# A gated DeltaNet scan with its chunk transitions formed ahead, on quarters of the array

## The chip, the cores and the metric

The kernel runs on one core of a Trainium2 chip. A core has a matrix engine (TensorE, PE in the profile), three engines for elementwise work (VectorE or DVE, ScalarE or ACT, GpSimd or POOL) and queues of DMA transfers. PE writes into PSUM, from which VectorE and ScalarE read; in this kernel POOL works on SBUF alone. The metric is the device time of one execution in microseconds: the median of several runs.

## The reference

Two layers of a transformer block over 256 context and 512 latent tokens of width 1024. Each layer modulates its input, projects it, sends parts of the projection through three mixers (a gated MLP over chunks, attention, a bidirectional gated DeltaNet), projects back, normalizes, and runs an MLP. The change is in the DeltaNet: 6 heads of 64 channels, run over the tokens in chunks of 64, once forward and once backward. For a head and a direction:

```python
sol = lax.linalg.triangular_solve(eye + lower, rhs, ...)     # rhs = [v * beta, k * beta * exp(gc)]
u, w = jnp.split(sol, 2, -1)
def step(s, inp):
    qd, kd, u_i, w_i, a_i, gl = inp
    v_new = u_i - w_i @ s
    o = qd @ s + a_i @ v_new
    s = s * jnp.exp(gl)[..., None, None] + kd.T @ v_new
    return s, o
s_final, o = lax.scan(step, state, xs)
```

`s` is the 64x64 state of the head, `gc` the running sum of the log decay in the chunk, `gl` its last value, `a_i` the masked and decayed product of queries and keys of the chunk. All is float32. The second layer needs no outputs for the context tokens.

## The kernel before

**Stages.** A layer runs an input projection with the gated MLP, then the projections of DeltaNet and attention (304 us ends that stage in layer 0, about 1458 us in layer 1), then a stage in which attention and the DeltaNet scans run side by side (304 to 576 us and 1458 to 1672 us, the scan stages below), and then the output projection and the MLP, which fill most of the rest.

**Order.** The kernel is written as streams: Python generators that yield after each step. `Flow.run` puts them into one order at build time: the stream whose last step ends first, by the rough prices of `Flow.cost`, goes on next. Each engine then runs its instructions in that order. A stream asks for PSUM with `self.psum(n)`: up to 512 columns come from four tiles called `mm`, more from two called `ax`. Attention, the modulation and the DeltaNet share them. In the scan stage the streams are `makes(p)` and `scans(p)` for the three head pairs p, the attention, `prep(2)`, and in layer 0 `mods` (products `modw,cz`).

**DeltaNet.** Heads go in pairs p = 0, 1, 2. Token tiles have 128 tokens, two chunks each. `dn_prep` (p) makes, for all six tiles, the decayed products of queries and keys (`A`) and the transposed inverses of the unit-triangular systems (`TT`). The inverse rests on a long serial chain of small VectorE operations on `Xx` and `tm`. `prep(0)` and `prep(1)` run beside the projections, `prep(2)` in the scan stage.

The scan of a pair of heads goes in six step pairs v. A step pair takes forward the two chunks of tile v, and backward the two of tile `_tb(v)`. So there are 18 step pairs in a layer, 36 in all. 30 of them also give outputs (need: all of layer 0, and v over 1 in layer 1). `dn_make` gets the operands of a step pair ready, and `dn_scan` runs its two steps.

**dn_make** scales keys and queries by token (`gs`, VectorE), transposes them on PE against `c_ident`, and copies the pieces (ScalarE) into 128x128 blocks `rW` and `rQ`; the keys of the update go into `rK` and half of the increments into `rU` (VectorE), the inverses into `rT` (four DMAs from `TT`), the query products into `rA` (ScalarE). In each block the two directions stand on the diagonal and the rest is zero. `ring` makes the blocks in four copies and clears the zero parts with 160 POOL memsets of 64x128 in all, 80 at the start of each scan stage.

**dn_scan** runs a step as a chain over three engines: PE `S,rW`; VectorE `rr = rU - ...`; PE `rr,rT`; ScalarE copy `vn`; PE `vn,rK`; two VectorE operations that give the next `S`. With need, PE then does `S,rQ` and `vn,rA`, and ScalarE (first direction at a tile) or VectorE (second) puts the result into `o`. Each product is 128x128x128, both heads' columns past each head's weights:

```python
            # both heads move past the weights of each: it keeps the array's clock up, and only a head's own product is used
            for h in range(2):
                mm(px[:, 64 * h : 64 * h + P], c2(r["W"], h), S0, start=True, stop=True)
```

In the trace such a product is two records of the same shape (`S,rW` has 144 products and 288 records); a transpose is one. All operations are issued through a helper, so nearly every record has line L206, and one tells them apart by tile names. `S,rW` is a product of the tiles S and rW; `c_ident,ape` and `ava,apT` are attention's transposes and products with values, `akh,qs` and `akl,qs` its scores, `ax<-kq` products of `dn_prep` on 64x64 quarters of the array.

Of the kernel before, what the change touches and what calls it, by code (L numbers as in the profile page):

```python
# [8 lines left out]
F32 = mybir.dt.float32  # L9
# [7 lines left out]
P = 128  # L17
# [7 lines left out]
NH = 6  # L25
# [14 lines left out]
class Flow:  # L40
    """Interleaves streams of work (generators that yield after each step) as they are traced. The engines run what is
    traced in order, so the stream whose last step ends first, by a rough cost of each instruction, goes on next. A stream
    yields a generator to start it, a key to wait until that key is in `done`, a tuple of classes of PSUM tiles to get,
    or the time to go on."""

    # wait for a result of the same engine, of another one
# [68 lines left out]
    def when(self, s):  # L115
        """the time a stream can go on, None while what it waits for is not there"""
# [11 lines left out]
    def run(self, *gens, side=(), drain=False):  # L128
        """until the streams gens end; those of side go on in the next run if they have not ended, or else with drain"""
# [37 lines left out]
    def step(self, gen, val, ahead):  # L167
        """one step of a stream, its instructions as if they were traced that much earlier"""
# [42 lines left out]
class _Core:  # L211
    """the engines, with a note of all that is issued to them"""
# [6 lines left out]
def _tb(v):  # L219
    """token tile whose chunks the backward direction takes at step pair v (the forward one takes tile v)"""  # L220
# [63 lines left out]
class K:  # L284
# [22 lines left out]
    def setup(self):  # L307
# [21 lines left out]
        nc.vector.memset(self.mhalf, -0.5)  # L329
        self.cz = cp.tile([P, KD, 32], F32, name="cz")  # L330
# [6 lines left out]
        # scratch in DRAM  # L337
# [7 lines left out]
    def store(self, out, in_):  # L345
        """a store, traced when the data is about to be there: loads keep a queue to themselves"""
# [6 lines left out]
    def psum(self, *ns):  # L353
        """PSUM tiles of n columns, to be dropped after their last use"""
# [12 lines left out]
    def feed(self, name, side, srcs, raw, parts, scale=None, hold=""):  # L367
        """a pool for weight units with the stream that loads and splits them"""
# [12 lines left out]
    def rsqrt(self, out, in_, n, scale=1.0, eps=EPS):  # L381
        """out = (in_ * scale + eps) ** -0.5 on [P, n]"""
# [68 lines left out]
    def mod_in(self, wt, bt, bufs):  # L451
        """shift and scale of the first layer's input, one half of the channels after the other"""
# [122 lines left out]
    def norm_act(self, out, x, n):  # L575
        """(x - mean) * rstd on the scalar engine"""
# [41 lines left out]
    def chan(self, unit, xh, xl, rng):  # L618
        """channel-major block: psum [P, tokens] for the token columns of rng"""
# [14 lines left out]
    def tokm(self, units, rows, w, c0, c1, t, xh, xl):  # L634
        """token-major block: psum [P, c1-c0] for token tile t; units[i] holds the k-rows rows[i], each w wide"""
# [31 lines left out]
# channel blocks of each half that the vector engine takes in the first modulation  # L667
# [3 lines left out]
class Kernel(K):  # L671
# [23 lines left out]
    def mix(self, l, xp, xh, xl, rest):  # L695
        """rest: pools of the layer before that its last streams use"""
# [5 lines left out]
        # gMLP: u channel-major, v token-major with the gates of the DeltaNet  # L702
# [75 lines left out]
        # the weights of the next phase come in meanwhile  # L778
# [6 lines left out]
        # DeltaNet: convolutions of all heads, preparation of the first pairs; attention: q, k, v; gate of the DeltaNet  # L785
# [61 lines left out]
        # attention proper beside the scans  # L847
# [14 lines left out]
        def makes(p):  # L862
            yield f"prep{l}{p}"
            yield f"conv{l}{3 * p + 2}"
            for v in range(6):
# [5 lines left out]
        def scans(p):  # L871
# [7 lines left out]
            for v in range(6):  # L879
                yield f"made{l}{p}{v}"  # L880
                yield from self.dn_scan(l, p, v, G, R[p % 2][v % 2], S, o)
# [60 lines left out]
    def att_tab(self, l, at):  # L942
        """rotary tables times the norm gains: [q|k, cos|sin, tile, channel]"""
# [14 lines left out]
    def qk_norm(self, l, t, h0, ps, at):  # L958
        """rms-norm and rotary of the q|k heads h0.. of token tile t, then channel-major"""
# [57 lines left out]
    def z_gate(self, l, t, ps):  # L1017
        """silu(z) times the gain of the DeltaNet's output norm"""
        nc, ap_ = self.nc, self.atmp
        pz, ps = ps, ps[:, 128:512]  # L1020
        if t == self.tiles[0]:
# [15 lines left out]
    def attention(self, l, at):  # L1037
        """scores of a head run ahead of the products of the head before"""
# [97 lines left out]
    def dn_conv(self, l, u, c0, r, qkv):  # L1136
        """q, k or v of a head pair from its projection r: convolution, silu, norms; token-major"""
# [11 lines left out]
        # outputs run over cb columns a..b  # L1149
# [15 lines left out]
        # acc is twice the silu; to token-major  # L1165
# [11 lines left out]
        else:  # L1177
            # sums of squares over the channels of each head
# [7 lines left out]
            # l2 norm of x = acc / 2 with its guard; q also carries 1/8  # L1186
# [15 lines left out]
    def dn_gates(self, l, gt, gp, dp, G):  # L1202
        """decay sums and rates of all heads, [P, direction, tile, head]"""
# [18 lines left out]
        # softplus(x) = max(x, 0) + log(1 + e^-|x|), the log as 2 atanh(e / (2 + e))  # L1222
# [714 lines left out]
```

## Time and profile before

| | |
|---|---|
| median of 3 runs (lowest to highest) | 2101.53 us (2100.57 to 2102.2) |
| span of the profiled execution | 2099.3 us |
| PE busy | 1944.5 us, 93% |
| VectorE busy | 1358.6 us, 65% |
| ScalarE busy | 921.4 us, 44% |
| POOL busy | 195.3 us, 9% |

The span lies 2.2 us under the median. Busy shares are means over stages with different limits, and the busy time of PE counts modelled ends: a group of four records of `vn,rA` has 0.61 us of busy time, while the next group starts 0.44 us after it. So a stretch in which PE shows as nearly full can still hold waits. The profile's windows give busy times and the granted TensorE clock by stretch; 1.00 is 2.4 GHz, 0.50 is 1.2 GHz.

### The profile page before, as it was taken

What the parts mean: (1) busy time and instruction counts of PE and PEld (TensorE: products, weight loads), DVE (VectorE), ACT (ScalarE), POOL (GpSimd) and SP (SyncE); (2) the same over time, 40 slices, a digit from 0 to 9 for tenths busy, and PEclk for the clock granted to TensorE, in tenths of its full rate; (3) what the DMA queues carried; (4) which work ended last, traced back from release to release, by engine and by line L of the source; (5) the groups of instructions that cost most, each with busy time, mean ns of one, the idle gap of its engine ahead of it and who ended that gap; (6) DMA issues with size and microseconds to landing.
All of it is one profiled execution on the core that took longest, in us unless ns stands there. A gap on an engine that the chain in (4) does not pass through costs nothing. (4 is left out here: it accounts for less than half of the span.)

```text
span 2099.3 us, 31005 instructions
## 1 busy us (share of the span) xinstructions
PE 1944.5 (93%) x11870; PEld 1601.5 (76%) x11870; DVE 1358.6 (65%) x2659; ACT 921.4 (44%) x1881; POOL 195.3 (9%) x375
## 2 busy tenths in 40 slices
PE   6999779989898999999999989997988889999998
PEld 2887655678777888888888778875877768788886
DVE  5578887865577436362457777889896485544555
ACT  4444346566645322322232265443866445422341
POOL 1111221010012000000000111122100010000001
PEclk8999989989999999999999979977999999999999
DMA  7311024312335424241445243110101434322231
GB/s 280 103 46 51 16 75 149 117 40 64 112 110 181 132 72 159 81 140 43 139 161 173 98 142 95 53 36 26 34 23 30 166 129 164 107 90 81 96 107 59
DMA packets 98240, 208.91 MB, mean 100 GB/s; under 512 B 30850, under 2 KB 45058, under 8 KB 98092
## 3 DMA queue, kind: packets, MB, share of 16 engines
q1 hardware_dynamic: 86956, 189.24, 27.9%
q10 hardware_dynamic: 11136, 17.70, 2.2%
q8 instruction: 93, 1.52, 0.3%
q14 instruction: 55, 0.45, 0.1%
HBM read 184.38 MB, written 17.79 MB: 96 GB/s over the span
## 5 line engine op out<-in xcount | busy, mean ns | idle before, releaser
L206 ACT ACTIVATE whi<-wraw 128x1024 fp32r<-128x1024 f32 (+2 forms) x188 | 194.9, 1050 | 440.6 <-PE ax L206 287.8
L206 DVE TENSOR_TENSOR wlo<-wraw,whi 128x1024 fp32r<-128x1024 f32 (+2 forms) x188 | 226.4, 1211 | 224.6 <-ACT whi L206 224.1
L206 PE MATMUL mm<-x2xh,whi 128*128 128x256 f32 (+1 forms) x832 | 288.4, 347 | 10.5 <-ACT whi L206 9.0
L206 PE MATMUL mm<-x2xh,wlo 128*128 128x256 f32 (+1 forms) x832 | 287.3, 346 | 1.6 <-DVE wlo L206 1.6
L206 PE MATMUL mm<-x2xl,whi 128*128 128x256 f32 (+1 forms) x832 | 287.7, 346 | 0.0
L206 PE MATMUL ax<-whi,hh 128*128 128x512 f32 x640 | 251.2, 392 | 0.0
L206 PE MATMUL ax<-whi,hl 128*128 128x512 f32 x640 | 250.0, 391 | 0.0
L206 PE MATMUL ax<-wlo,hh 128*128 128x512 f32 x640 | 249.9, 390 | 0.0
L206 PEld LDWEIGHTS mm<-x2xh,whi 128*128 128x128 f32 x832 | 158.9, 191 | 34.1 <-ACT whi L206 9.4
L206 DVE TENSOR_TENSOR acc<-acc,ax 128x1024 f32<-128x1024 f32 x68 | 82.9, 1219 | 148.3 <-PE ax L206 148.1
L206 PEld LDWEIGHTS mm<-x2xh,wlo 128*128 128x128 f32 x832 | 158.6, 191 | 22.6 <-DVE wlo L206 2.4
L206 PEld LDWEIGHTS mm<-x2xl,whi 128*128 128x128 f32 x832 | 158.8, 191 | 19.9
L206 PEld LDWEIGHTS ax<-whi,hh 128*128 128x128 f32 x640 | 120.2, 188 | 29.7 <-ACT hh L206 5.2
L206 PEld LDWEIGHTS ax<-whi,hl 128*128 128x128 f32 x640 | 120.1, 188 | 27.5 <-DVE hl L206 2.9
L206 PEld LDWEIGHTS ax<-wlo,hh 128*128 128x128 f32 x640 | 120.2, 188 | 27.0 <-issue 2.6
L206 ACT ACTIVATE rl<-mm 128x256 f32<-128x256 f32 (+1 forms) x104 | 50.7, 490 | 129.1 <-PE mm L206 123.7
L206 DVE SCALAR_TENSOR_TENSOR acc<-modw,cz,acc 128x1024 f32<-128x1024 f32 x80 | 101.2, 1280 | 8.4 <-DMA acc<-in_mod_b 5.4
L206 POOL TENSOR_SCALAR rs<-mv 128x1 f32<-128x1 f32 x52 | 33.1, 637 | 699.1 <-DVE mv L206 696.8
L206 PE MATMUL mm<-ava,apT 128*128 128x128 f32 x624 | 88.4, 285 | 2.7 <-ACT apT L206 1.2
L206 PEld LDWEIGHTS mm<-ava,apT 128*128 128x128 f32 x624 | 78.8, 197 | 7.2 <-ACT apT L206 3.2
L206 DVE TENSOR_TENSOR hl<-rl,hh 128x768 fp32r<-128x768 f32 (+2 forms) x76 | 54.4, 716 | 29.4 <-ACT hh L206 29.4
L206 DVE SCALAR_TENSOR_TENSOR cacc<-cb,cw,cacc 128x772 f32<-128x772 f32 (+1 forms) x72 | 69.7, 972 | 0.7 <-ACT cacc L206 0.2
(255 smaller groups left out, 4178.5 us busy)
## 6 DMA issues: line engine op xcount, KB each, us to landing
wraw<-in_w_up SPq DMA_DIRECT2D x64, 512.0 KB
wraw<-in_w_down SPq DMA_DIRECT2D x64, 512.0 KB
modw<-in_mod_w SPq DMA_DIRECT2D x56, 512.0 KB
modw<-in_mod_w SPq DMA_DIRECT2D x80, 256.0 KB
wraw<-in_w_ch SPq DMA_DIRECT2D x22, 512.0 KB
wraw<-in_w_out SPq DMA_DIRECT2D x16, 512.0 KB
x_d<-xt ACTq DMA_DIRECT2D x16, 512.0 KB
xt<-x_d SPq DMA_DIRECT2D x14, 512.0 KB
```

The source lines that it names most:

```text
L206: return f(*args, **kw)
```

## The change

The step is rewritten as one product and one addition: s' = P s + C, with the transition P = exp(gl) I - kd' w and the increment C = kd' u, and o = Q s + a u with the reading matrix Q = qd - a w. None of P, C, Q and a u depends on the state.

- `dn_make` scales keys and values on VectorE (`kv`, three operations) and ScalarE (one), and `kd`, `qd` and `ei` (the identity times the decay) on POOL (two operations each, 128x128). PE then does products of 64x64 weights on quarters of the array: `kv,TT` (8 per step pair, 128 columns) gives w and u in one; ScalarE copies them to `rwu`; then `kd,rwu` (8) and `rwu,kd` (8) give P and C, and `id,qd` (8) with `A,rwu` (8, accumulated) give Q, 64 columns each. VectorE adds `ei` (128x256), ScalarE copies C and Q.
- `dn_scan` does `rwu,A` (8) once per step pair, and per step four `S,rP` and, with need, four `S,rQ`, then one 128x128 VectorE addition for `S`. Both steps keep two `mm` tiles. At the end of the step pair ScalarE copies (128x256), VectorE adds (128x256) and POOL puts the two results into `o`.
- The padded blocks, their memsets and the DMAs of `rT` go. `A` becomes one tile, and `dn_prep` writes it with two 128x256 products per group of two token tiles where it had two of 64x256 and four of 64x128.
- `Flow.cost` prices products of 64x64 weights at 0.9 ns a column; the decays `E` come from one product instead of 24 small ones per layer; `makes(2)` waits for the last operands of p = 0; one VectorE operation more in the gates.

```diff
+            if m == 64 and ins[0].shape[0] == 64:
+                return 0.9 * n
...
     def dn_make(self, l, p, v, qkv, G, A, TT, r):
...
-            ps = yield from self.psum(256)
-            for h in range(2):
-                self.tr(ps[:, 128 * h : 128 * h + P], g_[:, h].rearrange("p d e -> p (d e)"))
...
-            nc.sync.dma_start(out=r["T"][f, :, 3 * hf, :], in_=T4[f, 0, v])
...
+        for d, t in enumerate(td):
+            mul(nc.vector, kv[:, d, :, 0, :], k[:, t], ks[:, d, t, hs])
+        nc.scalar.copy(kv[:, 0, :, 1, :], vv[:, v])
+        mul(nc.vector, kv[:, 1, :, 1, :], vv[:, td[1]], be[:, 1, td[1], hs])
+        for d, t in enumerate(td):
+            mul(nc.gpsimd, kd[:, d], k[:, t], kds[:, d, t, hs])
...
+        ps = yield from self.psum(512)
+        for d, h in blk:
+            for f in halves:
+                o = P * (2 * d + h)
+                mm(ps[f, o : o + P], T4[f, d, h, td[d]], kv[f, d, h].rearrange("p a b -> p (a b)"), start=True, stop=True)
...
+        nc.scalar.copy(wu.rearrange("p d h c -> p (d h c)"), ps)
...
+        ps, pc = yield from self.psum(512, 256)
+        for d, h in blk:
+            for i, f in enumerate(halves):
+                mm(ps[f, 256 * d + 64 * h : 256 * d + 64 * h + HD], wu[f, d, h, 0:HD], kd[f, d, h], start=True, stop=True)
+                e = i if d == 0 else 1 - i
+                o = P * e + 64 * h
+                mm(pc[halves[1 - i], o : o + HD], kd[f, d, h], wu[f, d, h, HD:P], start=True, stop=True)
...
+        nc.vector.tensor_tensor(out=r["P"], in0=pv[:, :, 0, :], in1=ei.rearrange("p d h c -> p d (h c)"), op=ALU.add)
+        nc.scalar.copy(r["C"].rearrange("p e c -> p (e c)"), pc)
...
+    def dn_scan(self, l, p, v, A, r, S, o):
...
+            for h, i, f, d in w:
+                c = P * e + 64 * h
+                mm(px[halves[1 - i], c : c + HD], r["P"][f, d, 64 * h : 64 * h + HD], S0[f, h, :], start=True, stop=True)
+            for h, i, f, d in w if need else ():
+                c = 256 + P * d + 64 * h
+                mm(po[f, c : c + HD], r["Q"][f, d, 64 * h : 64 * h + HD], S0[f, h, :], start=True, stop=True)
...
+            nc.vector.tensor_tensor(
+                out=S2.rearrange("p h c -> p (h c)"), in0=px[:, P * e : P * e + P], in1=r["C"][:, e, :], op=ALU.add
+            )
...
+        nc.scalar.copy(yo, y[:, 0])
+        nc.vector.tensor_tensor(out=yo, in0=yo, in1=y[:, 1], op=ALU.add)
...
+                nc.gpsimd.tensor_tensor(out=of[:, t], in0=of[:, t], in1=yo[:, d], op=ALU.add)
```

**PE, late in the scan stage of layer 1.** Before, one step with need stands so, among the scores and transposes of attention:

```order
L206 MATMUL mm_66<-S,rW_12546 128x128 x2
L206 MATMUL mm_68<-c_ident,gs 128x128 x2
L206 MATMUL mm_69<-c_ident,ape 128x128 x2
L206 MATMUL mm_66<-rr,rT_12551 128x128 x2
L206 MATMUL ax_70<-akh,qs 128x512
L206 MATMUL ax_70<-akl,qs 128x512
L206 MATMUL ax_70<-akh,qs 128x256
L206 MATMUL mm_66<-vn,rK_12556 128x128 x2
L206 MATMUL ax_70<-akl,qs 128x256
L206 MATMUL mm_67<-S,rQ_12561 128x128 x2
L206 MATMUL mm_67<-vn,rA_12566 128x128 x2
```

Now both steps of a step pair stand in a few rows, with the products `kv,TT` of a later step pair between them:

```order
L209 MATMUL mm_69<-ava,apT 128x128 x6
L209 MATMUL mm_67<-rwu_12781,A_12797 64x64 x8
L209 MATMUL mm_66<-S,rP_12782 64x64 x4
L209 MATMUL mm_67<-S,rQ_12783 64x64 x4
L209 MATMUL mm_68<-kv,TT_12798 64x128 x8
L209 MATMUL mm_66<-S,rP_12782 64x64 x4
L209 MATMUL mm_67<-S,rQ_12783 64x64 x4
L209 MATMUL mm_69<-c_ident,ape 128x128 x4
```

What moved: the three products that each waited for another engine became one round of quarter products per step, and PE changes between whole-array and quarter products there (110 stretches of 64x64 products in the program, 27 before).

**VectorE, in the projections of layer 1.** Before, a group of two token tiles of `dn_prep` writes `A` in six operations:

```order
L206 TENSOR_TENSOR A_11026<-ax_71,M 64x2x2x64 x2
L206 TENSOR_TENSOR A_11027<-ax_71,DB 64x2x64 x4
L206 TENSOR_TENSOR M<-ax_71,M 128x2x128 x2
L206 SCALAR_TENSOR_TENSOR cacc<-cb_11048,cw,cacc 128x772 x2
L206 TENSOR_TENSOR A_11027<-ax_71,M 64x2x2x64 x2
```

Now in two:

```order
L209 TENSOR_TENSOR A_11269<-ax_70,M 128x2x128
L209 TENSOR_TENSOR A_11269<-ax_70,DB 128x2x128
L209 TENSOR_TENSOR M<-ax_70,M 128x2x128 x2
L209 SCALAR_TENSOR_TENSOR cacc<-cb_11290,cacc 128x512
L209 SCALAR_TENSOR_TENSOR cacc<-cb_11289,cw,cacc 128x772
```

Only the operations on `A` are fewer; the convolution (`cacc`) and `M` stand beside them as before.

**POOL, at the start of the scan stage of layer 1.** Before, the stretch begins with the memsets of the states and of the padded blocks (20 rows of `x4`, of which the first stand here):

```order
L206 MEMSET S_12542 128x128
L206 MEMSET S_12543 128x128
L206 MEMSET rW_12546 64x2x64 x4
L206 MEMSET rT_12551 64x2x64 x4
L206 MEMSET rK_12556 64x2x64 x4
```

Now the operands of the step pairs follow the states:

```order
L209 MEMSET S_12777 128x128
L209 MEMSET S_12778 128x128
L209 MEMSET TT_12798 128x1536
L209 TENSOR_TENSOR kd<-qkv_11263,kds 128x128 x2
L209 TENSOR_TENSOR ei<-id_84,E 128x128 x2
L209 TENSOR_TENSOR qd<-qkv_11263,egc 128x128 x2
L209 TENSOR_TENSOR kd<-qkv_11264,kds 128x128 x2
```

The memsets of the ring are gone, and POOL's products stand where `dn_make` needs them, through the whole stage.

## Rows read from the trace of the kernel before

**Rows 1.** The page of the profile: its first line.

```profile
span 2099.3 us, 31005 instructions
```

**Rows 2.** Windows: stretch, length, PE, PEld, DVE, ACT, POOL busy (records), clock, DMA share, GB/s.

```profile
180.00:304.00 124.00, 105.19 (x711) 83.18 (x709) 108.83 (x240) 45.08 (x78) 18.19 (x19) 0.94 0.11 37
304.00:432.00 128.00, 118.09 (x911) 74.89 (x913) 98.23 (x343) 79.65 (x244) 17.97 (x89) 0.96 0.40 124
432.00:475.00 43.00, 38.66 (x387) 34.34 (x382) 26.04 (x91) 29.50 (x106) 5.09 (x4) 0.80 0.19 52
475.00:576.00 101.00, 92.31 (x717) 84.43 (x715) 56.89 (x169) 65.59 (x180) 2.47 (x2) 1.00 0.28 90
1370.00:1458.00 88.00, 77.63 (x548) 63.68 (x546) 75.10 (x181) 30.50 (x57) 16.81 (x21) 0.82 0.06 23
1458.00:1550.00 92.00, 78.64 (x792) 70.50 (x793) 84.38 (x278) 73.08 (x213) 16.08 (x82) 0.93 0.14 34
1550.00:1672.00 122.00, 99.88 (x895) 88.00 (x895) 74.61 (x242) 71.87 (x209) 5.51 (x6) 0.97 0.22 70
```

**Rows 3.** Records by tile, whole span: count, then duration ns min/median/max.

```profile
L206 PE MATMUL mm<-S,rW x288: 272/275/582, 315.5 to 1642.4; 128*128 128x128 f32 x144
L206 PE MATMUL mm<-S,rQ x240: 272/275/422, 324.7 to 1643.9; 128*128 128x128 f32 x120
L206 PE MATMUL mm<-c_ident,gs x132: 271/273/477, 310.9 to 1634.1; 128*128 128x128 f32 x132
```

**Rows 4.** Timeline of PE, full clock: start us, busy us, group of records.

```profile
377.81 0.61 PE L206 MATMUL mm<-vn,rA 128*128 128x128 f32 x4
378.35 0.66 PE L206 MATMUL ax<-kq 64*64 64x128 f32 x10
378.94 0.71 PE L206 MATMUL mm<-S,rQ 128*128 128x128 f32 x4
379.49 0.61 PE L206 MATMUL mm<-vn,rA 128*128 128x128 f32 x4
...
414.89 0.61 PE L206 MATMUL mm<-S,rW 128*128 128x128 f32 x4
415.33 0.61 PE L206 MATMUL mm<-ava,apT 128*128 128x128 f32 x4
```

**Rows 5.** Groups of instructions, 1458 to 1550 us: count, busy us, mean ns, idle before.

```profile
L206 DVE TENSOR_TENSOR rK<-qkv,kds 64x128 f32<-64x128 f32 x42 | 11.4, 282 | 0.4
L206 DVE SCALAR_TENSOR_TENSOR S<-S,E,mm 128x64 f32<-128x64 f32 x38 | 9.4, 275 | 3.5 <-PE mm L206 2.1 <-ACT o L206 0.6 <-ACT rU L206 0.5
```

**Rows 6.** Timeline of VectorE, one group of `dn_prep` in layer 1's projections.

```profile
1419.60 0.76 DVE L206 TENSOR_TENSOR M<-ax,M 128x256 f32<-128x256 f32 x2
1420.49 0.86 DVE L206 TENSOR_TENSOR A<-ax,M 64x256 f32<-64x256 f32 x2
1421.38 1.20 DVE L206 TENSOR_TENSOR A<-ax,DB 64x128 f32<-64x128 f32 x4
```

**Rows 7.** Waits, 1458 to 1672 us: engine, awaited, us in total, times, longest.

```profile
PE mm L206 <- DVE gs L206: 7.8, 2, 7.6
PE mm L206 <- ACT vn L206: 3.8, 9, 0.9
PE mm L206 <- DVE rr L206: 3.6, 5, 2.1
```

**Rows 8.** Records by tile, POOL, whole span.

```profile
L206 POOL MEMSET rK<- x32: 197/198/201, 306.8 to 1470.9; 64x128 f32 x32
L206 POOL TENSOR_SCALAR rs<-mv x52: 190/430/2252, 22.9 to 2092.4; 128x1 f32<-128x1 f32 x52
```

**Rows 9.** Windows before a fall of the clock and after it, columns as in Rows 2.

```profile
429.00:432.70 3.70, 1.94 (x61) 1.70 (x60) 3.65 (x8) 2.67 (x6) 0.00 (x0) 1.00 0.00 0
433.00:443.00 10.00, 10.00 (x102) 8.64 (x102) 4.92 (x21) 6.86 (x26) 0.00 (x0) 0.50 0.01 3
```

**Rows 10.** Timeline of PE in the second of these windows.

```profile
437.39 1.06 PE L206 MATMUL mm<-S,rW 128*128 128x128 f32 x4
```

More of the change, by code (lines that the diff above doesn't have):

```diff
@@ L329, in setup @@
         nc.vector.memset(self.mhalf, -0.5)
+        self.id2 = cp.tile([P, HD], F32, name="id2")
+        for f in range(2):
+            nc.vector.tensor_copy(self.id2[_half(f)], self.ident[_half(f), 64 * f : 64 * f + HD])
         self.cz = cp.tile([P, KD, 32], F32, name="cz")
@@ L864, in makes @@
             yield f"conv{l}{3 * p + 2}"
+            if p == 2:
+                yield f"made{l}05"
             for v in range(6):
@@ L1020, in z_gate @@
         pz, ps = ps, ps[:, 128:512]
+        yield f"z{l}{t - 1}" if t > self.tiles[0] else f"qk{l}{LT[-1]}"
         if t == self.tiles[0]:
@@ L1249, in dn_gates @@
         gc, egc, kds = (gp.tile(sh, F32, name=n) for n in ("gc", "egc", "kds"))
-        gks = gp.tile([P, 6, NH], F32, name="gks")
+        ks = gp.tile(sh, F32, name="ks")
         ps, pr = yield from self.psum(144, 768)
@@ L1364, in dn_prep @@
         for g in range(3):
-            need = A[g] is not None
+            a0 = 0 if l == 0 else 2
+            need = 2 * g >= a0
             nq = 2 if need else 1
@@ L1513, in dn_make @@
-        if A is not None:
-            yield from rows("Q", q, egc[:, 1])
-            for hf, f in halves:
-                nc.scalar.copy(r["A"][f, :, hf:4:2, :], A[f, v % 2])
-            yield
-    def dn_scan(self, l, p, v, G, r, S, o):
+        mul = lambda eng, o, a, s: eng.tensor_tensor(out=o, in0=a, in1=_col(s, HD), op=ALU.mult)
+        halves = [_half(f) for f in range(2)]
+        blk = [(d, h) for d in range(2) for h in range(2)]
+        mm = nc.tensor.matmul
+        T4 = TT.rearrange("p (d h t) c -> p d h t c", d=2, h=2)
@@ new lines, in dn_make @@
+        if need:
+            qd = new("qd", 2, 2, HD)
+            for d, t in enumerate(td):
+                mul(nc.gpsimd, qd[:, d], q[:, t], egc[:, d, t, hs])
+            yield
+        ei = new("ei", 2, 2, HD)
+        for d, t in enumerate(td):
+            nc.gpsimd.tensor_tensor(
+                out=ei[:, d], in0=self.id2.unsqueeze(1).broadcast_to([P, 2, HD]), in1=_col(E[:, d, t, hs], HD), op=ALU.mult
+            )
+        yield
+        ps = yield from self.psum(512)
[3 more added lines that the diff above has]
+                mm(ps[f, o : o + P], T4[f, d, h, td[d]], kv[f, d, h].rearrange("p a b -> p (a b)"), start=True, stop=True)
@@ new lines, in dn_make @@
+        for d, h in blk if need else ():
+            o = 256 * d + P + 64 * h
+            for f in halves:
+                mm(ps[f, o : o + HD], qd[f, d, h], self.id2[f], start=True, stop=False)
+            for f in halves:
+                mm(ps[f, o : o + HD], wu[f, d, h, 0:HD], A[f, d, h, td[d] - a0], start=False, stop=True)
+        yield
+        pv = ps.rearrange("p (d w c) -> p d w c", d=2, w=2)
+        nc.vector.tensor_tensor(out=r["P"], in0=pv[:, :, 0, :], in1=ei.rearrange("p d h c -> p d (h c)"), op=ALU.add)
@@ new lines, in dn_scan @@
+        halves = [_half(f) for f in range(2)]
+        if need:
+            px, po = yield from self.psum(256, 512)
+            for d in range(2):
+                for h in range(2):
+                    for f in halves:
+                        c = P * d + 64 * h
+                        mm(po[f, c : c + HD], A[f, d, h, td[d] - a0], r["wu"][f, d, h, HD:P], start=True, stop=True)
+        else:
+            px = yield from self.psum(256)
+        for e in range(2):
+            S0 = S[0]
+            w = [(h, i, f, i if e == 0 else 1 - i) for h in range(2) for i, f in enumerate(halves)]
+            for h, i, f, d in w:
[4 more added lines that the diff above has]
+                mm(po[f, c : c + HD], r["Q"][f, d, 64 * h : 64 * h + HD], S0[f, h, :], start=True, stop=True)
@@ L1554, in dn_scan @@
             S[0] = S2
-            self.drop(px)
             yield
-            if need:
-                po = yield from self.psum(256)
-                y = po.rearrange("p (h c) -> p h c", c=HD)[:, 0:4:3, :]
-                for w, m in (("Q", S0), ("A", vf)):
-                    for h in range(2):
-                        mm(po[:, P * h : P * h + P], c2(r[w], h), m, start=(w == "Q" and h == 0), stop=(w == "A" and h == 1))
-                yield
-                for t, hf in ((v, e), (_tb(v), 1 - e)):
-                    f = _half(hf)
-                    dst = o[f, t]
-                    if v == 0 or v in (2, 3):
-                        nc.scalar.copy(dst, y[f])
-                    else:
-                        nc.vector.tensor_tensor(out=dst, in0=dst, in1=y[f], op=ALU.add)
-                self.drop(po)
-                yield
+        self.drop(px)
@@ new lines, in dn_scan @@
+        if not need:
+            return
+        y = po.rearrange("p (w d c) -> p w d c", w=2, d=2)
+        of = o.rearrange("p t h c -> p t (h c)")
+        yo = sc.tile([P, 2, P], F32, tag=f"yo{p % 2}", bufs=1, name="yo")
+        nc.scalar.copy(yo, y[:, 0])
+        nc.vector.tensor_tensor(out=yo, in0=yo, in1=y[:, 1], op=ALU.add)
+        self.drop(po)
+        yield
+        for d, t in enumerate(td):
+            if v == 0 or v in (2, 3):
+                nc.gpsimd.tensor_copy(of[:, t], yo[:, d])
+            else:
+                nc.gpsimd.tensor_tensor(out=of[:, t], in0=of[:, t], in1=yo[:, d], op=ALU.add)
```

128 lines of the change are left out of this document (35 added, 93 removed).

## The prediction

> **What bounds the kernel now.** I first took the windows of the stages that hold DeltaNet work [rows 2]. In the projections VectorE is ahead of PE or level with it (108.8 of 124 us, 75.1 of 88). In layer 0's scan stage, 304 to 576 us, PE leads: 118.1 + 38.7 + 92.3 = 249.1 of 272 us, so 22.9 us idle. In layer 1's, the first part (1458 to 1550) belongs to VectorE, 84.4 of 92 us with PE at 78.6; the second (1550 to 1672) belongs to nobody: PE 99.9 of 122, VectorE 74.6. A chain sets the pace there. The waits of that stage [rows 7] name it: PE waits for `vn` and `rr`, 7.4 us in all, hops of the step. The largest, 7.8 us for `gs`, is one stall at the stage's start. The other stages hold none of the changed work and stay as they are. So the change is worth something in four places: PE in layer 0, VectorE and then PE in layer 1's first part, the chain in the second, and VectorE in the projections.
>
> **PE's work.** A group of four 128x128x128 records, two products, starts 0.44 us before the next [rows 4], so a record takes 0.11 us. `S,rW` has 288 records [rows 3], 8 per step pair; by the code `rr,rT` and `vn,rK` have as many, and `vn,rA` as many as `S,rQ` (240, 8 per step pair with need). `gs` has 132 transposes, 4 per step pair with need, else 2. That is 44 x 0.11 = 4.84 us with need, 26 x 0.11 = 2.86 without.
>
> After, all are 64x64 quarters. The nearest row is `kq`: five products of 64x64 weights and 128 columns [rows 4]. They start 0.10 us later than the end of the group before them (377.81 + 0.44), and the next group starts 0.59 us after them. The group after that comes 0.55 us later where 0.44 is usual. So a change to quarters and back costs about 0.28 us (0.10 in, 0.09 out, taken as the entry, and 0.10 behind it), and five products stream in 0.50 us, 0.10 each. One by one they would take 0.22 each: about 2.2 quarters stream at a time. A product of 64 columns I take as half, 0.05. With need: 8 `kv,TT` x 0.10, and 8 each of P and C, 16 of Q, 8 of `rwu,A` and 16 in the steps, 56 x 0.05: 0.80 + 2.80 = 3.60 us. Without: 0.80 + 24 x 0.05 = 2.00. The order shows 83 more stretches of quarters than before, 2.3 per step pair, x 0.28 = 0.65. Sums: 4.25 and 2.65. PE saves 0.59 x 30 + 0.21 x 6 = 19 us, 10.6 in layer 0 and 8.4 in layer 1. That is little, since PE trades few padded products for many small ones. The bounds are far apart. If all four quarters stream at once, streaming falls to 3.60 x 2.2/4 = 1.98 and 1.10, and the saving grows by 1.62 x 30 + 0.90 x 6 = 54 us; if they stream one by one, it becomes 7.92 and 4.40, 144 us more than my value. I stay at 2.2, the only row of the same kind.
>
> **VectorE's work.** A 64x128 or 128x128 operation takes 0.28 us [rows 5]. With need there are 18 before (four `gs`, two `rU`, four `rK`, two `rr`, four `S`, and two adds to `o` on average), 5.0 us; now three `kv` and two `S` at 0.28 and two of 128x256 at 0.4 [rows 6], 2.2 us. Without need 3.9 becomes 1.8. In layer 1's first part about 10 step pairs run (42 `rK` rows, four each [rows 5]), so VectorE loses about 10 x 2.5 = 25 of its 84 us there, and PE, 78.6 less some 5, becomes the bound. The stall for `gs` at the start stays: its successor `kv` waits for the same chain `Xx`, `tm` on VectorE. 92 us become 74 + 8 = 82: **-10**.
>
> **The chain.** A step had five hops between engines; now it has two. In layer 1's second part PE saves its share, 8.4 x 8/18 = 3.7 us, and its half of the 7.4 us of waits [rows 7], 3.7; the attention that is left fills the rest as before, with idle time of its own. I take **-8**. In layer 0 PE saves 10.6, and of its 22.9 us idle I take as much per step pair as in layer 1, 7.4 us; attention and `modw,cz` already fill many of these holes, so two thirds, 5: **-16**.
>
> **The projections.** `A` took 0.86 + 1.20 = 2.06 us per group and will take about the 0.76 of `M`'s two operations of that shape [rows 6]: -1.3. Three groups lie in 180 to 304 us and two in 1370 to 1458, where VectorE leads: **-6**. The other groups lie beside work that PE sets or are in the part above. The 24 small products for `E` and the extra gate operation go at nothing: they stand early in the projections beside transfers and VectorE's work, a microsecond if not.
>
> **POOL.** It loses 160 memsets of 0.198 us [rows 8] at two stage starts, and gains 8 operations of 128x128 per step pair. No row shows such an operation. From the memset, 0.2, up to the longest `rs`, 2.25 [rows 8], I take 0.4, nearer to the memset, as most `rs` rows take 0.43. That is 3.2 us in a step pair that has 272/18 = 15 us in layer 0: hidden behind attention, since operands are made two step pairs ahead. At 2.25 it is 18 us, and POOL would be the bound.
>
> The spread of `rs` is contention: the same 128x1 operation takes 0.19 or 2.25 us. The Trainium skill ("SBUF — State Buffer", Who interferes with whom) says that a VectorE instruction with two SBUF inputs and a GpSimd instruction that reads SBUF exclude each other for their whole length; the spread agrees, and by that rule some of the 264 new operations wait for `wlo` or the like, and VectorE for them.
>
> I take **+4** for such waits, and for two `mm` tiles of four being held through a step pair while attention asks for them.
>
> **The clock.** At half level a group of four records shows 1.06 us where it shows 0.61 otherwise [rows 4, 10]. The clock fell at 433 us after a stretch in which PE was busy 1.94 of 3.70 us, and stayed at 1.2 GHz through 10 us in which it showed as fully busy [rows 9]. More 64-column work on parts of the array makes such stretches likelier; the code's own remark on both heads' columns speaks for it. In the scan stages the mean is 0.80 to 1.00 now [rows 2]. I take **+6**, some 12 us more at half level.
>
> **The sum.** -10 - 8 - 16 - 6 + 4 + 6 = -30. The profiled span is 2099.3 us [rows 1], the median 2.2 above it: 2069.3 + 2.2, about **2071 us**. Its own range: with half of the gain of four quarters at once 2044; with contention and clock at three times my values (+20) and half of PE's saving (+9) 2100.
>
> **Rivals.**
> (a) Half clock, slower. The scan stretches of quarter products pull the clock down and hold it there. Work done at 1.2 GHz costs half of its time there in excess. The forecast allows 12 us of such time; the gain of 30 is used up at 60 us more. The stretches with step pairs are 304 to 475 and 1458 to 1655, 368 us; a quarter of it, 92 us, gives 2071 + 46 - 6, about 2111 us. For it: the fall at 433 came in just such a mixture of small products. Against it: attention's whole-array products stand between them, and 475 to 576 ran at 1.00 [rows 2].
> (b) Quarters one by one: +144 on PE, 2215 us. Against it is the `kq` row.
> (c) Four quarters at once. P and C lie on different quarters, so more than two can overlap. PE saves up to 54 us more; where attention's own chain leaves PE waiting, 60% of it shows: 2071 - 32 = 2039 us, less if the clock stays up as well. The Trainium skill ("TensorEngine Tiling (Array Packing)", Key Properties) says tiles work independently and in parallel, which would make it four; the row shows 2.2, and it decides.
> (d) The freed time isn't on the path: attention sets the end of both stages, POOL's operations come late, and only the projections and the start gain: 2101.5 - 8 + 6, about 2099 us.
>
> **Chances.** Forecast 0.55, (c) 0.13, (d) 0.12, (a) 0.17, (b) 0.03. The range reaches into (a) and (c): 2034 to 2112. About 0.2%, 4 us, is what a measurement of this kernel can tell from no change. Faster by more than that: nearly all of the forecast, (c), a third of (d): 0.70. The same: the rest of (d) and a little of the forecast, 0.09. Slower: 0.21.
>
> **What the profile after would show.** PE: groups of `kd,rwu` and `S,rP` at about 0.05 us a product, stretches changing at 0.28 us; the scan stages near 256 and 196 us (before 272 and 214); granted clock there about 0.95. VectorE in the first part of layer 1's stage no longer above PE. POOL's products near 0.4 us, with nobody waiting for them. The forecast is wrong if windows of the scan stages show 0.50 for tens of microseconds, if `S` or `kv,TT` wait for POOL, or if quarters stream one by one.

## The result, and the profile after

| | before | after |
|---|---|---|
| median of 4 runs (lowest to highest) | 2101.28 us (2100.57 to 2102.2) | 2047.49 us (2046.79 to 2054.54) |
| span of the profiled execution | 2099.3 us | 2044.9 us |

The ratio is 0.9755 (95%: 0.9738 to 0.9771). The change makes the kernel about 54 us faster by the medians, 51 by the ratio. The forecast was 30 us, and the time lies inside its range. The page of the changed kernel, first line and busy times, against [rows 1]:

```profile
span 2044.9 us, 35399 instructions
...
PE 1889.7 (92%) x14526; PEld 1548.8 (76%) x14526; DVE 1273.9 (62%) x2225; ACT 855.7 (42%) x1587; POOL 279.0 (14%) x479
```

To place the gain, I compare the start of the same instruction in both traces: the first memset of the states (a scan stage of layer 0 begins), the first output-projection record `whi,yh` (it ends), the last record but three of `whi,xmxh`, a product of the projections of layer 1 (its scan stage begins). After the change a wait for `PB`, of the inverses, stands ahead of the last three such products, so the states' memset in layer 1 is a second mark for the same place.

| mark | before, us | after, us | shift, us |
|---|---|---|---|
| scan stage of layer 0 begins | 304.9 | 301.2 | -3.7 |
| it ends | 575.9 | 530.0 | -45.9 |
| scan stage of layer 1 begins | 1454.0 | 1408.8 | -45.2 |
| first memset of the states in layer 1 | 1457.0 | 1419.9 | -37.1 |
| scan stage of layer 1 ends | 1669.4 | 1609.9 | -59.5 |
| end | 2099.3 | 2044.9 | -54.4 |

So layer 0's scan stage gives 42 us, layer 1's 14, and the last 435 us give 5 back. With the memset as the mark, the wait counts to the projections: layer 1's stage gives 22, and its projections give 9 back. The split holds for one execution. Five variants below are no slower (`A` in six operations, `E` from 24 small products, independent steps, scans without a lead, the filled hole); in their traces layer 0's stage takes 229 to 234 us and layer 1's, from the mark `whi,xmxh`, 191 to 199, where it is 229 and 201 here. Windows of the two scan stages, columns as in [rows 2], first of the kernel before, between these marks (the last one from the memset, for a later comparison):

```profile
304.90:575.90 271.00, 248.69 (x1994) 193.29 (x1987) 180.16 (x600) 173.81 (x526) 25.31 (x95) 0.95 0.32 100
1454.00:1669.40 215.40, 179.39 (x1691) 159.17 (x1690) 160.01 (x530) 143.69 (x421) 22.56 (x93) 0.95 0.19 55
1457.00:1669.40 212.40, 176.47 (x1678) 157.10 (x1678) 157.32 (x521) 143.64 (x421) 22.54 (x93) 0.95 0.19 54
```

Then of the changed kernel, with the first 92 us of layer 1's stage behind them:

```profile
301.20:530.00 228.80, 208.09 (x3320) 159.32 (x3320) 141.05 (x385) 131.91 (x357) 74.46 (x158) 0.99 0.33 108
1409.00:1609.90 200.90, 169.74 (x2927) 143.41 (x2925) 126.38 (x341) 115.89 (x293) 58.09 (x133) 0.90 0.16 50
1409.00:1501.00 92.00, 78.31 (x1599) 65.26 (x1599) 63.99 (x170) 53.51 (x132) 39.70 (x91) 0.85 0.08 26
```

PE is busy 41 us less in layer 0 and only 10 us less in layer 1, and the clock is a reason: 0.95 became 0.99 in the one and 0.90 in the other. Read in windows of one microsecond, 27.3 us of layer 0's stage ran at 1.2 GHz before and 6.8 do now; in layer 1's it was 20.5 and is 40.9. Half of such time is lost: about 10 us won in one layer and 10 lost in the other. The sizes are this execution's: in the traces of the five variants, 7 to 19 us stand at 1.2 GHz in layer 0 and 23 to 31 in layer 1. VectorE, 84.4 of 92 us in layer 1's first part before [rows 2], has 64.0 now, under PE's 78.3, as forecast.

The quarter products stand in PE's timeline like this (start us, busy us, records; layer 0, full clock; the left-out rows carry on the same pattern):

```profile
444.13 0.40 PE L209 MATMUL ax<-akl,qs 128*128 128x512 f32 x1
444.46 0.27 PE L209 MATMUL mm<-kd,rwu 64*64 64x64 f32 x1
...
444.57 0.22 PE L209 MATMUL mm<-rwu,kd 64*64 64x64 f32 x1
444.58 0.22 PE L209 MATMUL mm<-kd,rwu 64*64 64x64 f32 x1
444.59 0.22 PE L209 MATMUL mm<-rwu,kd 64*64 64x64 f32 x1
444.63 0.22 PE L209 MATMUL mm<-kd,rwu 64*64 64x64 f32 x1
...
444.98 0.29 PE L209 MATMUL mm<-id,qd 64*64 64x64 f32 x4
445.09 0.29 PE L209 MATMUL mm<-A,rwu 64*64 64x64 f32 x4
445.21 0.29 PE L209 MATMUL mm<-id,qd 64*64 64x64 f32 x4
...
446.01 0.66 PE L209 MATMUL mm<-c_ident,ape 128*128 128x128 f32 x4
```

In P and C (`rwu,kd` and `kd,rwu`), four records start within 0.02 us, and the next four 0.058 us later, which is 0.029 us a product of two records. A padded record of 128 columns takes 0.11 us [rows 4], so one of 64 columns by itself would take about half of that: all four quarters run at once. In Q (`id,qd` with `A,rwu`), four records take 0.116 us, 0.058 us a product: two at once. The whole group of 64 records takes 1.55 us.

Waits of PE in the two scan stages (engine, awaited, us in total, times, longest), layer 0 and then layer 1, against [rows 7]:

```profile
...
PE mm L209 <- DVE S L209: 2.9, 3, 2.4
PE mm L209 <- POOL kd L209: 2.2, 1, 2.2
```

```profile
PE ax L209 <- DVE PB L209: 5.3, 1, 5.3
PE ax L209 <- DVE zg L209: 4.1, 3, 2.3
PE mm L209 <- ACT apT L209: 3.9, 6, 1.1
PE mm L209 <- ACT rwu L209: 2.9, 3, 1.3
...
PE mm L209 <- DVE S L209: 1.1, 2, 0.8
```

The waits for `gs`, `vn` and `rr` are gone, and the new step's own wait, for `S`, is 4.0 us in the whole program. The longest wait is no longer the scan's: `PB` belongs to the inverses of `dn_prep`, `apT` to attention. The hops inside the new `dn_make` remain, though: PE's waits for `kd`, `qd`, `rwu`, `rP`, `rC` and `rQ` come to about 7 us in each of the two stages. POOL's new products (records by tile, ns min/median/max) took what I had taken, 0.4 us:

```profile
L209 POOL TENSOR_TENSOR kd<-qkv,kds x72: 393/399/1122, 302.8 to 1568.0; 128x128 f32<-128x128 f32 x72
L209 POOL TENSOR_SCALAR rs<-mv x52: 190/482/2249, 23.3 to 2038.0; 128x1 f32<-128x1 f32 x52
```

### The profile page after: what moved, and what is told of

The parts are those of the page before. It is cut to its first block, busy times and chain, and to the rows that moved or that the text cites. A ratio compares the mean times of both kernels' runs of the same rounds, so it can differ in the third digit from the quotient of the medians.

```text
span 2044.9 us, 35399 instructions
## 1 busy us (share of the span) xinstructions
PE 1889.7 (92%) x14526; PEld 1548.8 (76%) x14526; DVE 1273.9 (62%) x2225; ACT 855.7 (42%) x1587; POOL 279.0 (14%) x479
## 5 line engine op out<-in xcount | busy, mean ns | idle before, releaser
L209 POOL MEMSET acc<- 128x1024 f32 x10 | 9.5, 955 | 469.3 <-PE mm L209 458.1
```

The costliest lines, as they stand in the source:

```text
L209: return f(*args, **kw)
```

## The experiments

Ratios are to the kernel before on the same chip, with 95% intervals. The five variants named above came out at 0.9728 to 0.9732, so a difference of a quarter per cent from 0.9755, some 5 us, tells nothing here; measured from those five, the losses below would be some 5 us larger. The planner follows each step's inputs and prices, so an edit can also change the order of the instructions. An edit is to the changed kernel unless it says otherwise, and rows of three dots stand for lines of it that are left out.

**More hops.** The sum of the step goes over ScalarE and POOL before VectorE adds.

```diff
...
+            nc.scalar.copy(h1, px[:, P * e : P * e + P])
...
+            nc.gpsimd.tensor_copy(h2, h1)
...
-                out=S2.rearrange("p h c -> p (h c)"), in0=px[:, P * e : P * e + P], in1=r["C"][:, e, :], op=ALU.add
+                out=S2.rearrange("p h c -> p (h c)"), in0=h2, in1=r["C"][:, e, :], op=ALU.add
```

> The changed kernel with two more hops in each of the 72 steps: before the addition for S, ScalarE copies the product out of PSUM and POOL copies that copy (128x128 each). TensorE's and VectorE's work is the same. Theory H (the gain of 54 us comes from the shorter chain between engines): with four hops in place of two of the five before, half of the gain or more is lost, 2070 to 2085 us. Theory P (the gain is TensorE's own time, 113 to 81 us in layer 0's stage): within 6 us of 2047.

2056.5 us, 0.9787 (0.9762 to 0.9811): 7 us over the changed kernel, not far above the noise, a little over what theory P allowed and far from theory H. The hops were real; of VectorE's addition (records by tile, and below it how long VectorE sat idle before it and how often):

```profile
L209 DVE TENSOR_TENSOR S<-h,rC x72: 254/292/476, 315.2 to 1585.3; 128x128 f32<-128x128 f32 x72
...
  POOL h L209: 42.6, 52
```

VectorE waited 42.6 us for the hops, and PE filled nearly all of it with other work. So the chain of the steps hardly sets the pace any more.

**P and C twice.**

```diff
-        for d, h in blk:
+        for d, h in blk + blk:
```

> The changed kernel with the 16 products for P and C of each step pair issued twice: 16 x 0.05 x 36 = 29 us more of TensorE's time, none for another engine and no new hop. Theory P: TensorE's time is the path nearly everywhere, so 2067 to 2076 us. Theory H: TensorE has room beside the waits, 2047 to 2055 us.

2070.22 us, 0.9860 (0.9826 to 0.9894): 22 us more. The group of `rwu` products grew from 1.55 to 2.03 us, 0.47 x 36 = 17 us. The other 5 us are no more than the noise. So PE's time in these products comes through whole, as theory P had it.

**Neighbours on one quarter.** The same products, with the loop over halves outermost, so that records that follow each other lie on the same quarter. All lists of quarter products were changed so; this is the one of P and C.

```diff
...
-        for d, h in blk:
-            for i, f in enumerate(halves):
+        for i, f in enumerate(halves):
+            for d, h in blk:
...
```

> The changed kernel with every list of quarter products in another order: all that use one quarter of the array first, then those of the next, so that neighbours share a quarter. Same products, same other engines. If products stream two or more at a time only because neighbours lie on different quarters, a step pair with need takes up to 7.9 us of TensorE in place of 3.6: 2115 to 2190 us. If records of one quarter overlap as well or TensorE has room, 2047 to 2065 us.

2113.3 us, 1.0063 (1.0042 to 1.0084): 65 us more, 13 us slower than the kernel before and just under the first range. PE's timeline of it, columns as above:

```profile
460.71 0.50 PE L209 MATMUL mm<-kd,rwu 64*64 64x64 f32 x5
...
461.05 0.22 PE L209 MATMUL mm<-kd,rwu 64*64 64x64 f32 x1
461.11 0.22 PE L209 MATMUL mm<-rwu,kd 64*64 64x64 f32 x1
461.11 0.22 PE L209 MATMUL mm<-kd,rwu 64*64 64x64 f32 x1
461.17 0.22 PE L209 MATMUL mm<-rwu,kd 64*64 64x64 f32 x1
...
462.26 0.28 PE L209 MATMUL mm<-A,rwu 64*64 64x64 f32 x2
462.38 0.28 PE L209 MATMUL mm<-id,qd 64*64 64x64 f32 x2
...
463.69 0.49 PE L209 MATMUL mm<-ava,apT 128*128 128x128 f32 x2
```

Two records per 0.058 us instead of four in P and C, two per 0.116 instead of four in Q; the group takes 2.98 us instead of 1.55. That is 1.43 x 30 = 43 us in the step pairs with need. The other lists slow too: 16 records of `kv,TT` in one group take 1.48 us in the median at full clock, where they took 0.97 to 1.02. The clock adds to it in layer 0, 0.92 against 0.99, but not in layer 1, 0.92 against 0.90:

```profile
307.90:575.70 267.80, 254.87 (x3320) 204.39 (x3320) 140.04 (x383) 133.14 (x357) 70.30 (x158) 0.92 0.29 92
1468.70:1681.10 212.40, 191.11 (x2866) 169.14 (x2864) 118.57 (x321) 112.66 (x285) 58.95 (x132) 0.92 0.14 46
```

The changed kernel gains because neighbours in its order of products lie on different quarters; with the same products in this order it would have been a loss.

**POOL's products on VectorE.** `kd`, `qd`, `ei` and the writes to `o`, 264 operations, of which the edit shows the first.

```diff
-            mul(nc.gpsimd, kd[:, d], k[:, t], kds[:, d, t, hs])
+            mul(nc.vector, kd[:, d], k[:, t], kds[:, d, t, hs])
...
```

> The changed kernel with the 264 operations that it gave to POOL (kd, qd, ei and the writes to o) on VectorE: 264 x 0.28 = 74 us more for VectorE, 106 us less for POOL. Theory V (part of the gain is VectorE's relief, above all in layer 1): 2060 to 2075 us. Theories H and P: VectorE has room since the change, 2042 to 2054 us; a gain would mean that POOL's operations were late or in VectorE's way.

2051.27 us, 0.9757 (0.9728 to 0.9785): no difference, although VectorE is at 80.7 of the first 92 us of layer 1's stage again:

```profile
1427.70:1519.70 92.00, 78.66 (x1581) 65.39 (x1579) 80.74 (x268) 55.44 (x134) 5.01 (x9) 0.89 0.08 26
```

VectorE's load and the contention with POOL together are worth nothing measurable; the run doesn't part the two.

**`A` in six operations.** `A` keeps its new layout, and the six shapes of before write it.

```diff
-                    out=A[:, dd, :, 2 * g - a0 : 2 * g - a0 + 2, :], in0=pv[:, :, :, 1, :], in1=m4((M[:, 0], DB)[dd])[:, :, ts_, :], op=ALU.mult
+                        out=A[_half(hf), 0, :, 2 * g - a0 : 2 * g - a0 + 2, :], in0=pv[_half(hf), :, :, 1, :],
+                        in1=m4(M[:, 0])[_half(hf), :, ts_, :], op=ALU.mult,
...
+                            out=A[_half(hf), 1, :, 2 * g - a0 + i, :], in0=pv[_half(hf), :, i, 1, :],
+                            in1=m4(DB)[_half(hf), :, 2 * g + i, :], op=ALU.mult,
```

> The changed kernel with A written as before, in two operations of 64x256 and four of 64x128 per group where the change has two of 128x256: 15 x 1.2 = 18 us more for VectorE, six of them in stretches where the prediction had VectorE on the path. The prediction's term: +6 us. The trace's marks (the projections' end moved by under 1 us in either layer against their start): 0 to +2 us.

2045.64 us, 0.9731 (0.9706 to 0.9756): nothing. In the changed kernel, the two operations on `A` save nothing that can be measured.

**`E` from 24 small products.**

```diff
-        nc.tensor.matmul(ps, self.sel.rearrange("p a b -> p (a b)"), fl(g), start=True, stop=True)
...
+        for t in range(6):
+            for dd in range(2):
+                for f in range(2):
+                    nc.tensor.matmul(pv[_half(f), dd, t, :], self.sel[:, f, :], g[:, dd, t, :], start=True, stop=True)
```

> The changed kernel with the 24 products of 6 columns for the decays E per layer in place of one: the prediction priced them at nothing. By the trace, records after them come 3.5 to 6 us earlier in layer 0 since the change, and about 1 us in layer 1: +3 to +7 us. If the 5 us came from the clock's phase alone: within 2 us.

2044.29 us, 0.9732 (0.9707 to 0.9757): nothing that can be told from the noise.

**The kernel before, with its scaling on POOL.** `gs`, `rK` and half of `rU` leave VectorE.

```diff
-        mul = lambda o, a, s: nc.vector.tensor_tensor(out=o, in0=a, in1=_col(s, HD), op=ALU.mult)
+        mul = lambda o, a, s: nc.gpsimd.tensor_tensor(out=o, in0=a, in1=_col(s, HD), op=ALU.mult)
```

> The kernel before with the scalings of dn_make (gs, rK and half of rU) on POOL: VectorE is relieved of up to ten operations per step pair, 2.8 us, as much as by the change; TensorE's products and the chain stay. Theory V (VectorE's relief is what the change gained in layer 1, and part of it in layer 0): 2075 to 2088 us. Theories P and W: 2096 to 2106 us, or slower where the transposes wait for POOL at 0.4 us an operation.

2134.23 us, 1.0154 (1.013 to 1.0178): 32 us slower. VectorE has 124.2 us in layer 1's stage where it had 157.3, and PE waits for POOL instead (layer 1's stage):

```profile
PE mm L206 <- POOL gs L206: 17.0, 6, 9.8
```

The clock is lower there too, 0.89 where it was 0.95. As a test of VectorE's relief the run is spoilt by this, and it doesn't tell what the relief alone is worth.

**The kernel before, without the waits inside a step.** `rr`, `vn` and the new `S` no longer read what the product before them wrote. All instructions stay, but the planner puts them into another order.

```diff
-            nc.vector.tensor_tensor(out=rr, in0=r["U"][:, :, e, :], in1=x0, op=ALU.subtract)
+            nc.vector.tensor_tensor(out=rr, in0=r["U"][:, :, e, :], in1=r["U"][:, :, e, :], op=ALU.add)
...
-            nc.scalar.copy(vn, x1)
+            nc.scalar.copy(vn, rr)
...
-                    out=S2[:, h, :], in0=S[0][:, h, :], scalar=E[:, v, e, 2 * p + h : 2 * p + h + 1], in1=x0[:, h],
+                    out=S2[:, h, :], in0=S[0][:, h, :], scalar=E[:, v, e, 2 * p + h : 2 * p + h + 1], in1=r["U"][:, h, e, :],
```

> The kernel before with the waits inside its steps taken out: rr is rU added to itself, vn is copied from rr, and S takes rU, so that no operation of a step reads a product of that step. All products, copies and additions are still issued, with the same shapes; the DeltaNet's values are not computed. Theory W (about 23 us of the gain are waits of TensorE for the other engines in the chain): 2070 to 2085 us. Theory P (the gain is TensorE's streaming, the waits are covered by attention): 2092 to 2102 us.

2074.86 us, 0.9873 (0.9849 to 0.9897): 27 us (22 to 32) from the waits, with the order that the planner chose without them; the run doesn't part the two. Its windows of the two scan stages, against 271.0 and 212.4 us before:

```profile
304.00:559.60 255.60, 236.96 (x2000) 186.31 (x2000) 179.93 (x601) 175.40 (x527) 25.46 (x95) 0.97 0.35 106
1440.90:1641.60 200.70, 168.14 (x1680) 155.91 (x1680) 157.18 (x521) 144.97 (x420) 22.16 (x92) 0.95 0.20 58
```

15.4 us in layer 0, of which the clock gave about 7 (27.3 us at half level became 13.7), and 11.7 in layer 1 at an unchanged clock. There PE runs as many records (1680, 1678 before) and is busy 8.3 us less (176.5 to 168.1), while its idle time falls by 3.4: most of the wait had stood under busy time.

**The changed kernel, with its steps independent.** Each step reads the first state.

```diff
-            S[0] = S2
```

> The changed kernel with every step reading the first state of its head pair: the addition still waits for its product, but no step waits for the step before it. All products, copies and additions are issued; the DeltaNet's values are not computed. Theory W as e9_cut left it (the chain cost the kernel before 27 us, and the change removed most of that): 2035 to 2048 us, a ratio of 0.970 to 0.976. If the chain costs as much as before and only its products got cheaper: 2020 to 2030 us, 0.962 to 0.967.

2042.99 us, 0.9729 (0.9707 to 0.9751): 4.5 us by the medians, within the noise. What is left of the chain is too little to measure.

**Two turns of the planner.** The inverses of the third head pair (`prep(2)`) are planned five times as far ahead; or the scans get no lead.

```diff
-        flow.run(*chains, self.attention(l, at), [prep(2), BIAS], *([mods()] if full else []), drain=True)
+        flow.run(*chains, self.attention(l, at), [prep(2), 5 * BIAS], *([mods()] if full else []), drain=True)
```

> The changed kernel with prep(2) five times as far ahead of attention in the planner's order (5000 ns for 1000), which moves the chain of Xx and tm in the scan stage and with it p = 2's step pairs earlier. If layer 1's stage waits for prep(2) (attention alone runs through its last 30 us, after step pairs that wait for prep(2)): 2030 to 2042 us. If TensorE's work sets the stage: 2043 to 2053 us.

2074.21 us, 0.9870 (0.9846 to 0.9893): 24 us slower, outside both ranges. The loss lies in layer 0's scan stage, 252.6 us where it was 228.8; layer 1's is 3.5 us longer (its windows, from the same marks as those of the changed kernel):

```profile
301.30:553.90 252.60, 219.74 (x3320) 164.65 (x3320) 142.76 (x387) 132.28 (x357) 72.03 (x158) 0.95 0.30 97
1432.90:1637.30 204.40, 167.26 (x2928) 142.84 (x2926) 131.76 (x342) 116.16 (x293) 59.97 (x133) 0.90 0.15 50
```

Some 8 us of it are clock (0.95 against 0.99). PE also waits longer for the step and for a transfer there (waits of PE in layer 0's stage):

```profile
PE mm L209 <- DVE S L209: 6.8, 6, 2.7
...
PE mm L209 <- DMA modw<-in_mod_w: 4.0, 7, 1.1
```

The rest is open. The order alone can thus cost as much as the waits of the chain did.

```diff
-        chains = [[f(p), BIAS] for p in range(3) for f in (scans, makes)]
+        chains = [[f(p), 0.0] for p in range(3) for f in (scans, makes)]
```

> The changed kernel with no lead for the DeltaNet streams over attention in the planner's order (0 ns for 1000; prep(2) keeps its lead). The step is so short now that it may need none: if attention waits for PSUM tiles that step pairs hold, 2035 to 2045 us; if the chains then end later than attention, 2050 to 2065 us.

2044.15 us, 0.9731 (0.9712 to 0.9749): not told apart from the change.

**Filling the clock's hole.** Layer 1's scan stage begins with a wait, and the clock falls behind it (windows of the changed kernel, columns as in [rows 2]):

```profile
1407.80:1414.60 6.80, 2.79 (x13) 1.98 (x11) 6.42 (x17) 1.17 (x4) 0.00 (x0) 1.00 0.15 55
1414.60:1435.00 20.40, 16.30 (x251) 12.97 (x253) 16.33 (x36) 14.99 (x32) 12.13 (x24) 0.50 0.16 53
```

So 24 products of the identity were put ahead of `PB,M`, to keep PE busy through the wait.

```diff
...
+        if l == 1 and p == 1:
+            for _ in range(24):
+                nc.tensor.matmul(pz[:, 0:P], self.ident, self.ident, start=True, stop=True)
...
```

> The changed kernel with 24 products of the identity with itself (128x128x128, 24 x 0.22 = 5.3 us of TensorE) put ahead of the products PB,M of prep(1) in layer 1, where TensorE waited 5.3 us for VectorE and the clock then stood at 1.2 GHz for 20.5 us (1414.6 to 1435.0). Their results are not used. If that wait made the clock fall and whole-array products keep it up: no half level there, and 5 to 10 us less, a ratio of 0.968 to 0.973 to the kernel before. If the quarter products behind it bring the clock down by themselves: half level in the same stretch all the same, 2044 to 2052 us.

2041.09 us, 0.9728 (0.9702 to 0.9753): not told apart from the change, and the edit missed its place. The products ran at 1399 to 1401 us, before the wait, which stayed (PE's timeline; in brackets the idle time before a row, and what ended it):

```profile
1408.57 0.39 PE L209 MATMUL mm<-whi,xmxh 128*128 128x512 f32 x1
1415.77 1.46 PE L209 MATMUL ax<-PB,M 32*32 32x32 f32 x47 [6.82 <-ACT zth L209]
```

The clock fell behind it again, for 6.8 us, and once more for the 10.2 us of the second window here:

```profile
1407.10:1413.90 6.80, 1.85 (x9) 1.20 (x7) 6.39 (x18) 0.76 (x2) 0.00 (x0) 1.00 0.15 58
1427.50:1437.70 10.20, 7.43 (x136) 6.21 (x131) 9.71 (x22) 6.11 (x13) 8.64 (x15) 0.50 0.10 27
```

That filling the wait would keep the clock up was therefore not tried.

## Why the prediction was right, and where its sizes were off

The direction and the main mechanism held: PE's own time falls, the chain of hops goes, and nothing takes its place. The gain is 54 us where 30 were forecast. By the steps:

**PE's work: right.** Forecast were 4.25 us per step pair with need. Measured at full clock: `kv,TT` 1.02, the P, C and Q group 1.55, `rwu,A` with its step 0.85, the other step 0.41, and about 0.1 for each of the 2.3 entries, together some 4.1. The saving is about 0.7 x 30 + 0.4 x 6 = 23 us against 19, and P and C twice says that such time shows whole. Inside, errors nearly cancelled: P and C run four at once, nearly twice as fast as I took, while Q took 0.058 us a product, not 0.05, and `kv,TT` 0.13, not 0.10. I let the `kq` row [rows 4] decide between two quarters and four; it speaks for Q, and not for P and C, whose neighbours lie on four. The Trainium skill ("TensorEngine Tiling (Array Packing)", Key Properties) says that tiles work independently and in parallel; for P and C the trace agrees, 0.058 us for four records. Rival (c) was half true, for the cheaper half.

**The chain: the step that failed.** For its waits I had 3.7 us in layer 1 and 5 in layer 0, about 9. Cut in the kernel before, they gave 27 us, about 20 without the clock's part: 12 in layer 1 and 9 in layer 0, in the order that the planner then chose. I took them from the waits that the profile names [rows 7] and from the time in which PE showed as idle [rows 2], 22.9 us in layer 0. Both leave out what lies under the modelled ends of records: a group of four shows 0.61 us, and its place is 0.44 [rows 4]. My own note on the profile said so, and the sum did not use it. With the waits cut, PE's busy time in layer 1 fell by 8.3 us and its idle time by 3.4.

**Layer 1's first part, VectorE: right in what is seen, not in the reason.** VectorE went from 84.4 to 64.0 us of 92 and lies under PE. But 264 operations back on VectorE cost nothing, with VectorE at 80.7 of 92 us, so its relief was not shown to be worth the 10 us that I gave it. The 18 us of both parts of layer 1's stage came out as 14 (17 to 25 in the traces of the five variants), from PE's work (0.7 x 12 + 0.4 x 6 = 11) and waits (12), less the clock's 10.

**Layer 0: -16 forecast, -42 measured.** PE's work (0.7 x 18 = 13), waits (9) and clock (10) make 32 of it. The other 10 us are not explained; among what is left are the waits in `dn_make`, which no run cut, and the order. In the traces of the five variants the stage gives 37 to 42 us.

**Projections: -6 forecast, none shown.** Layer 0's scan stage starts 3.7 us earlier in this trace, at 301.2 us where it was 304.9. But in the traces of the eight variants that leave layer 0's projections as they are it starts anywhere from 301.3 to 308.0. Layer 1's projections gain nothing (-45.9 where layer 0's scan stage ends, -45.2 near their end), and neither `A` in six operations nor the small products of `E` cost anything when put back.

**POOL: +4 forecast, nothing measurable.** The price of 0.4 us was right, 0.399 in the median. PE waited for `kd` 3.0 us in the whole program, and moving all 264 operations away gave nothing. The other part of this term, two `mm` tiles held through a step pair, no run tested.

**Clock: +6 forecast, about 0 measured in the scan stages, as +10 and -10.** The sign of rival (a), tens of microseconds at half level, stands in layer 1, 41 us in this trace, and the opposite in layer 0. The direction is the same in the traces of the five variants (27.3 us became 7 to 19 in layer 0, 20.5 became 23 to 31 in layer 1); the sizes are not, and what decides it per stage is open. Of the last 5 us that the output side gives back, clock is a part too: 0.96 before and 0.92 now in the 90 us after the scan stage, 0.04 x 2 x 90 / 2 = 3.6 us (windows of before, then of after):

```profile
1669.40:1759.50 90.10, 79.32 (x432) 67.33 (x433) 67.45 (x90) 51.67 (x93) 10.88 (x16) 0.96 0.51 178
```

```profile
1609.90:1700.00 90.10, 76.32 (x403) 64.32 (x404) 64.17 (x86) 48.94 (x86) 11.08 (x16) 0.92 0.47 162
```

**Rivals (b) and (d)** fell: quarters do not run one by one in this order, and freed time on PE and in the chain both reached the end.

**In sum**, that the time lay in the range rests on PE's work, which held, and on the chain, which went the right way and was twice as large as I took it. Part of it is luck: -6 for the projections, the part of -10 that VectorE's relief was to bring, +4 and +6 were none of them shown, and in the sum they nearly cancel.

## What to carry to other kernels

A chain's waits can hide under modelled ends: compare the starts of successive groups with the spacing that such groups have when nothing is waited for, or cut the waits in a run that leaves the instructions, and look whether their order stayed as well. When products are put on quarters of the array, the order in which they are issued is part of the design: neighbours on different quarters were worth 65 us here. An engine that shows as nearly full need not be on the path: VectorE at 80.7 of 92 us cost nothing here.

## What was not expected of the hardware

- Four 64x64 quarters at once: four records of 64 float32 columns per 0.058 us when neighbours in the order of issue lie on four quarters, and two per 0.058 us (P and C) or per 0.116 us (Q) when products of one quarter stand together.
- The clock stayed low for long: after 6.8 us in which PE was busy 2.79 us came 20.4 us at 1.2 GHz, with PE busy 16.3 of them, on small products. Whether the wait or the products behind it keep it low, no run shows.
- Whether 264 operations of 0.3 to 0.46 us ran on POOL, beside VectorE's work, or on VectorE itself could not be measured in the time.
